# A transformer trunk on one core: V products with the high parts first, one four-bank score tile, a factor from two scalars

## The chip, the core and the metric

The kernel runs on one core of a Trainium2 chip. The metric is the device time of one execution in microseconds (us), taken as the median of several runs. Five engines work side by side, each through its own instructions in order: PE (TensorE, the matrix products), ACT (ScalarE), DVE (VectorE), POOL (GpSimd) and SP (SyncE, which issues the DMAs). They wait for one another by semaphores.

## The reference, cut to what matters

The program is a trunk of two layers over 1024 tokens of width 1024, in fp32. Each layer is a token mixer and a gated feed-forward block (SwiGLU), both behind a modulated RMS norm. The change touches the mixer of the first layer, differential attention, and one helper that both mixers use.

```python
def block(qi):                       # 128 queries, 8 heads, 2 components of width 64
    s = einsum('bqhcd,bkhcd->bhcqk', qi, k)
    p = softmax(s, axis=-1)
    w = p[:, :, 0] - lam * p[:, :, 1]
    return einsum('bhqk,bkhe->bqhe', w, v)
...
o = rmsnorm(o, subln_g) * (1.0 - lam_init)
return o @ w_o
```

The second layer's mixer is grouped-query attention with 8 heads and an ordinary softmax.

## The kernel before

**Products.** An fp32 operand is split into a high and a low part of a shorter type (`split`, L94: ACT casts the high part, another engine subtracts it to get the low one). A product is then three matmuls: high by high, high by low, low by high. That is why a projection tile of 128x512 over 1024 inputs takes 24 matmuls (`mm3`, L105 to L107).

**Units of the first layer's attention.** `layer0_attn` walks 64 units: 8 heads by 8 blocks of 128 queries. A unit has these steps.
- `diff_scores` (L532 on): 12 score matmuls (L548) into two tiles "S" of [128, 1024] fp32, one for each component, two PSUM banks each. Then, for each component, its negated maximum over the keys (L556, DVE), for component 0 a shift by a logarithm (L558, DVE), and the exponential with its row sum (L559, ACT).
- Still in `diff_scores`: the reciprocal of component 1's sum (L563), the factor rho = sum0 * (-lambda) / sum1 (L564), and e0 + rho * e1 in one pass (L565), all on DVE.
- `p_transpose` (L251): two groups of four 128x128 transposes (L256) into a bank "T", and the split of each (ACT cast L95, DVE subtraction L96) into the tiles `pt`.
- `av` (L262), once for two units: 24 matmuls of 256 columns into a half of bank "A" (L268 to L270). For every block k of keys it does V high by P high, V low by P high, V high by P low.
- `subln` (L568), once for four units: A copied to SBUF (L573, ACT), squared (L574), row sums by PE into A (L184), a chain of small operations on four columns (L579 to L589, DVE and one POOL), a broadcast by PE (L190), and the scaled result (L591).

Between these steps the PE computes the next head's Q, K and V projections, 144 matmuls a head into the single bank "M", which ACT evacuates (L470). For Q and K a rotary embedding follows (`rope`: L221 on DVE, L223 to L225 on POOL, then a split). Once a head V is transposed, eight 128x128 blocks (L242). Modulation vectors of the layer come from POOL (L129) and ACT (L130), spread over the units.

**PSUM before.** Eight banks: four in the pool `pss` (two tiles "S"), two "T", one "A", one "M". The two "S" tiles serve one unit; the next unit's scores go into the same two. `issue_after` keeps all other score matmuls of a unit behind its first.

**What sets the order.** The Python code issues the units with a look-ahead of two (`attention`, L272, with the order string "spatpup" for this layer). A scheduler then orders every engine's instructions by priorities (`high_priority` with offsets) and by its own forecast of times, and places the waits by tile: an instruction that reads or writes a tile is ordered against the others that touch that tile. So the order on an engine isn't read from the source, but from the compiled program.

A **turn**, below, is four units, which is half a head: two `av`, one `subln`, 72 projection matmuls. It falls into four stretches, each from the end of one unit's scores to the end of the next unit's. They are called A to D here: in A the second `av` of a group and, once a head, the V transposes; in B the row sums and the first steps of `subln`, then projections; in C the broadcast, projections and the beginning of the next group's first `av`; in D the rest of that `av`, then projections. After the change all 24 products of that `av` stand in C, and D has projections alone beside its transposes.

Of the kernel before, what the change touches and what calls it, by code (L numbers as in the profile page):

```python
# [12 lines left out]
ALU = mybir.AluOpType  # L13
AX = mybir.AxisListType

P = 128
S = 1024
D = 1024
KT = 8
NF = 22  # L20
CH = 512
# [19 lines left out]
PSUM = bass.MemoryType.PSUM  # L41
# [17 lines left out]
class Trunk:  # L59
# [144 lines left out]
    def norm_apply(self, pool, xs, rb, av, bv, hs):  # L204

        nc = self.nc

        def step(d):
            u = self.t(pool, "ft", [P, CH])
            b = bv[:, d:d + 1]  # L210
            nc.vector.scalar_tensor_tensor(out=u, in0=xs[d], scalar=av[:, d:d + 1], in1=rb, op0=ALU.mult, op1=ALU.mult)
            hi, lo = hs[d] = self.hpair()
            nc.scalar.activation(out=hi, in_=u, func=AF.Identity, bias=b, scale=1.0)
            nc.vector.scalar_tensor_tensor(out=lo, in0=u, scalar=b, in1=hi.bitcast(F32), op0=ALU.add, op1=ALU.subtract)  # L214

        return [lambda d=d: step(d) for d in range(KT)]
# [45 lines left out]
    def av(self, v, pt, ps):  # L262
        mm = self.nc.tensor.matmul
        vh, vl = v
        for k in range(KT):
            ks = slice(k * P, (k + 1) * P)
            hi, lo = pt[k // 4][0][:, k % 4, :], pt[k // 4][1][:, k % 4, :]
            mm(ps, lhsT=vh[:, ks], rhs=hi, start=(k == 0), stop=False)  # L268
            mm(ps, lhsT=vl[:, ks], rhs=hi, start=False, stop=False)  # L269
            mm(ps, lhsT=vh[:, ks], rhs=lo, start=False, stop=(k == KT - 1))  # L270

    def attention(self, units, fills, part1, part2, after, order, depth=2):  # L272

# [24 lines left out]
    def run(self):  # L298
        tc, nc, a = self.tc, self.nc, self.a
        with tc.tile_pool(name="cp", bufs=1) as cp, tc.tile_pool(name="sp", bufs=2) as sp, \  # L300
                tc.tile_pool(name="hp", bufs=50) as hp, \
                tc.tile_pool(name="pss", bufs=2, space=PSUM) as pss, \
                tc.tile_pool(name="pst", bufs=2, space=PSUM) as pst, \
                tc.tile_pool(name="psa", bufs=1, space=PSUM) as psa, \
                tc.tile_pool(name="psm", bufs=1, space=PSUM) as psm:
            self.cp, self.sp, self.hp, self.pss = cp, sp, hp, pss
            self.banks = {"T": pst, "A": psa, "M": psm}
            sm = self.sm = cp.tile([P, C_END], F32, name="sm")
            nc.sync.dma_start(out=sm, in_=a["small"])
            self.ident = cp.tile([P, P], F32, name="ident")  # L310
            make_identity(nc, self.ident)
            self.ones = cp.tile([P, 1], F32, name="ones")
            nc.vector.memset(self.ones, 1.0)
            self.nhalf = cp.tile([P, 8], F32, name="nhalf")
            nc.vector.memset(self.nhalf, -0.5)
            self.cond = cp.tile([P, 8], F32, name="cond")
            nc.scalar.activation(out=self.cond, in_=sm[:, C_C:C_C + 8], func=AF.Silu)
            self.mods = [[cp.tile([P, 8], F32, name=f"mod{i}_{j}") for j in range(6)] for i in range(2)]
            self.avec = [[cp.tile([P, 8], F32, name=f"a{i}_{j}") for j in range(2)] for i in range(2)]
            o_dram = [self.dram(f"o{i}") for i in range(2)]  # L320
            x_dram = self.dram("xs")

            with tc.tile_pool(name="wp0", bufs=2) as self.wp, tc.tile_pool(name="cr", bufs=1) as self.cpool:
                hs, proj0 = self.start()
                ow = self.layer0_attn(hs, proj0, o_dram[0])
            hs = self.ffn(0, ow, x_dram)
            with tc.tile_pool(name="wp1", bufs=2, reuse_waits="tile") as self.wp:
                ow = self.layer1_attn(hs, o_dram[1], x_dram)
            self.ffn(1, ow, None)

    def dram(self, name):
        return self.tc.dram_tile([KT, P, S], F32, name=name)

    def start(self):

        nc, a = self.nc, self.a
        m, av = self.mods[0], self.avec[0][0]
        hs = [[None] * KT, [None] * KT]
        S0, S1 = self.t(self.pss, "S"), self.t(self.pss, "S")
        accs = [[S0[:, :CH], S0[:, CH:]], [S1[:, :CH], S1[:, CH:]], [self.bank("T"), self.bank("M")]]  # L340
        with self.tc.tile_pool(name="st", bufs=2) as st, self.tc.tile_pool(name="stx", bufs=8) as stx, \
                self.tc.tile_pool(name="stw", bufs=1) as stw, \
# [189 lines left out]
    def diff_scores(self, q, k, u, ep, s4):  # L532
        nc = self.nc
        es = []
        s1 = self.t(self.sp, "sum", [P, 1])
        sums = [s4[:, u % 4:u % 4 + 1], s1]
        us = slice(u % 4 * P, (u % 4 + 1) * P)
        qh, ql = q[u // 4]
        pss = [self.t(self.pss, "S") for _ in range(2)]
        first = None  # L540

        for n in range(2):
            kh, kl = k[n]
            for i, (x, y) in enumerate(((qh, kh), (qh, kl), (ql, kh))):
                for c in range(2):
                    r = slice(c * 64, c * 64 + 64)
                    with self.tc.issue_after(first.ins) if first else contextlib.nullcontext():
                        ins = nc.tensor.matmul(pss[c][:, n * CH:(n + 1) * CH], lhsT=x[r, us], rhs=y[r, :], start=i == 0, stop=i == 2)  # L548
                    if n == i == 0:
                        first = ins  # L550
        for c in range(2):
            ps = pss[c]
            mx = self.t(self.sp, f"mx{c}", [P, 1])
            e = self.t(ep, "e")
            with self.tc.high_priority(offset=SAHEAD):
                nc.vector.tensor_reduce(out=mx, in_=ps, op=ALU.max, axis=AX.X, negate=True)  # L556
                if c == 0:
                    nc.vector.tensor_scalar(out=mx, in0=mx, scalar1=self.lnbig, scalar2=None, op0=ALU.subtract)  # L558
                nc.scalar.activation(out=e, in_=ps, func=AF.Exp, bias=mx, scale=1.0, accum_out=sums[c])  # L559
            es.append(e)  # L560
        rho = self.t(self.sp, "rho", [P, 1])
        with self.tc.high_priority(offset=SAHEAD):
            nc.vector.reciprocal(out=rho, in_=s1)  # L563
            nc.vector.scalar_tensor_tensor(out=rho, in0=sums[0], scalar=self.neglam, in1=rho, op0=ALU.mult, op1=ALU.mult)  # L564
            nc.vector.scalar_tensor_tensor(out=es[0], in0=es[1], scalar=rho, in1=es[0], op0=ALU.mult, op1=ALU.add)  # L565
        return es[0]

# [181 lines left out]


    def norm_parts(self, ft, bslot, tmp, xs, rb, av, bv, c, h0, ops):

        nc = self.nc
# [449 lines left out]
```

## Time and profile before

| | us |
|---|---|
| median of 3 runs | 2755.31 (2752.56 to 2761.1) |
| the profiled execution, its own time | 2753.28 |
| its span in the trace | 2751.2 |
| PE busy | 2600.1 (95%) |
| DVE busy | 1913.9 (70%) |
| ACT busy | 1193.2 (43%) |
| POOL busy | 988.7 (36%) |

The span is the time between the first and the last instruction in the trace; the execution's own time is 2.1 us longer. The first layer's attention takes about 100 to 745 us of the span, the second layer's about 1560 to 1990 us; the rest is the start and the two feed-forward blocks. Starts in the trace are us from the start of the span. A matmul's duration in the trace overlaps the next one's, so that the pace is read from the starts.

### The profile page before, as it was taken

To read this page: it belongs to the slowest core of one execution; us is meant where nothing else is said; L and a number is where in the kernel's file an instruction comes from. 1 tells how busy PE (TensorE), PEld (TensorE's weight loads), DVE (VectorE), ACT (ScalarE), POOL (GpSimd) and SP (SyncE) were. 2 spreads that over 40 slices of the span, in tenths; PEclk is the share of its full clock that TensorE was granted. 3 is DMA by queue.
4 is the path that set the end of the run, shared out by engine and by line. 5 is a ranking of instruction groups with operands and counts; after the bars stand their busy time and mean duration, and the time that the engine had idled before them with its cause. 6 is when DMAs were issued, how large, how long until landed. Compare 5 with 4: busy or idle time off the path is not lost.

```text
span 2751.2 us, 34376 instructions
## 1 busy us (share of the span) xinstructions
PE 2600.1 (95%) x12888; PEld 2138.1 (78%) x12888; DVE 1913.9 (70%) x2921; ACT 1193.2 (43%) x2049; POOL 988.7 (36%) x664
## 2 busy tenths in 40 slices
PE   6799999999998999999999899999998999999997
PEld 5577777777776888888887788888877888888886
DVE  6777777777667667676666777577567666666666
ACT  5455555555443333333334565555443333332323
POOL 7634444531154223232223456433153222222222
PEclk9899999999998999999999999999999999999998
DMA  6211211112211222221214222213211111111112
GB/s 255 74 44 49 70 50 59 63 42 96 78 49 58 66 65 74 65 69 62 71 64 146 96 73 89 85 59 110 70 35 50 54 50 58 54 50 54 50 58 85
DMA packets 86582, 195.89 MB, mean 71 GB/s; under 512 B 9488, under 2 KB 11792, under 8 KB 86416
## 3 DMA queue, kind: packets, MB, share of 16 engines
q1 hardware_dynamic: 86416, 193.71, 20.7%
q8 instruction: 101, 1.65, 0.3%
q14 instruction: 65, 0.53, 0.1%
HBM read 177.94 MB, written 15.73 MB: 70 GB/s over the span
## 4 chain that ended last, share of the span: by engine, by line
PE 76%; DVE 12%; ACT 3%; POOL 3%; DMA 2%; issue 2%; SPq 0%; DVEq 0%; ACTq 0%; POOLq 0%
PE T L105 7%; PE T L106 7%; PE T L107 7%; PE S L106 6%; PE S L105 6%; PE S L107 6%; PE M L105 6%; PE M L106 5%; PE M L107 5%; PE S L548 3%; PE T L256 3%; PE A L270 2%; PE A L268 2%; PE A L269 2%; DVE mx L556 2%
## 5 line engine op out<-in xcount | busy, mean ns | idle before, releaser
L833 POOL TENSOR_TENSOR raw<-raw,raw 128x512 f32<-128x512 f32 x214 | 299.2, 1399 | 877.5 <-DMA raw<-in_w_in 552.1
L95 ACT CAST whi<-raw 128x512 fp32r<-128x512 f32 x402 | 249.0, 621 | 672.1 <-PE T L106 215.7
L96 DVE TENSOR_TENSOR wlo<-raw,whi 128x512 fp32r<-128x512 f32 x402 | 330.3, 826 | 124.8 <-ACT whi L95 124.4
L105 PE MATMUL M<-h,whi 128*128 128x512 f32 x616 | 252.6, 410 | 8.6 <-ACT tmp L470 4.2
L1036 DVE SCALAR_TENSOR_TENSOR h<-T,mod,h 128x512 f32<-128x512 f32 (+1 forms) x270 | 197.7, 733 | 70.8 <-PE T L107 69.6
L107 PE MATMUL M<-h,wlo 128*128 128x512 f32 x616 | 244.6, 397 | 1.0 <-POOL wlo L96 1.0
L105 PE MATMUL S<-h,whi 128*128 128x512 f32 x572 | 226.7, 397 | 19.5 <-DVE ft L918 19.3
L106 PE MATMUL M<-h,whi 128*128 128x512 f32 x616 | 244.9, 398 | 0.0
L95 ACT CAST pt<-T 128x512 fp32r<-128x512 f32 x256 | 145.3, 588 | 211.5 <-PE T L256 211.0
L106 PE MATMUL S<-h,whi 128*128 128x512 f32 x572 | 227.5, 398 | 5.0 <-DVE h L214 3.1
L96 DVE TENSOR_TENSOR pt<-T,pt 128x512 fp32r<-128x512 f32 x256 | 171.6, 682 | 80.7 <-ACT pt L95 80.4
L107 PE MATMUL S<-h,wlo 128*128 128x512 f32 x572 | 226.2, 396 | 0.0
L105 PE MATMUL T<-g,whi 128*128 128x512 f32 (+1 forms) x540 | 210.7, 390 | 10.2 <-DVE h L1036 8.8
L106 PE MATMUL T<-g,whi 128*128 128x512 f32 (+1 forms) x540 | 208.3, 386 | 1.4 <-DVE g L96 1.4
L107 PE MATMUL T<-g,wlo 128*128 128x512 f32 (+1 forms) x540 | 207.9, 385 | 0.0
L129 POOL TENSOR_TENSOR wraw<-wraw,cond 128x1024 f32<-128x1024 f32 x64 | 155.9, 2437 | 126.9 <-DMA wraw<-in_ada_t 119.6
L556 DVE TENSOR_REDUCE mx<-S 128x1 f32<-128x1024 f32 x128 | 150.2, 1215 | 44.3 <-PE S L548 44.2
L270 PE MATMUL A<-pt,v 128*128 128x256 f32 x512 | 155.6, 304 | 23.2 <-DVE pt L96 23.2
L559 ACT ACTIVATE e<-S,mx 128x1024 f32<-128x1024 f32 x128 | 141.4, 1111 | 71.7 <-DVE mx L558 71.7
L256 PE MATMUL T<-ident,e 128*128 128x128 f32 x1024 | 149.1, 280 | 13.3 <-DVE pt L96 10.1
L268 PE MATMUL A<-pt,v 128*128 128x256 f32 x512 | 156.3, 305 | 4.3 <-ACT pt L95 4.2
L269 PE MATMUL A<-pt,v 128*128 128x256 f32 x512 | 151.4, 296 | 0.0
(290 smaller groups left out, 6445.7 us busy)
## 6 DMA issues: line engine op xcount, KB each, us to landing
raw<-in_w_in SPq DMA_DIRECT2D x200, 256.0 KB, 2.8
wraw<-in_ada_t SPq DMA_DIRECT2D x64, 512.0 KB, 3.2
raw<-in_w_out SPq DMA_DIRECT2D x88, 256.0 KB, 2.6
wraw<-in_wqkvA SPq DMA_DIRECT2D x23, 512.0 KB, 3.2
aq<-in_ada_s SPq DMA_DIRECT2D x16, 512.0 KB, 4.9
raw<-in_ada_w SPq DMA_DIRECT2D x32, 256.0 KB, 2.6
wraw<-in_wqkvB SPq DMA_DIRECT2D x15, 512.0 KB, 3.3
o<-tmp SPq DMA_DIRECT2D x28, 256.0 KB, 2.0
```

The costliest lines, as they stand in the source:

```text
L95: self.nc.scalar.copy(out=hi, in_=src)
L96: (eng or self.nc.vector).tensor_tensor(out=lo, in0=src, in1=hi.bitcast(F32), op=ALU.subtract)
L105: mm(ps, lhsT=whi[:, ws], rhs=xh, start=first and k == 0, stop=False)
L106: mm(ps, lhsT=whi[:, ws], rhs=xl, start=False, stop=False)
L107: mm(ps, lhsT=wlo[:, ws], rhs=xh, start=False, stop=last and k == n - 1)
L256: nc.tensor.transpose(ps[:, i * P:(i + 1) * P], w[:, k * P:(k + 1) * P], self.ident)
L268: mm(ps, lhsT=vh[:, ks], rhs=hi, start=(k == 0), stop=False)
L269: mm(ps, lhsT=vl[:, ks], rhs=hi, start=False, stop=False)
L270: mm(ps, lhsT=vh[:, ks], rhs=lo, start=False, stop=(k == KT - 1))
L556: nc.vector.tensor_reduce(out=mx, in_=ps, op=ALU.max, axis=AX.X, negate=True)
L833: self.nc.gpsimd.tensor_tensor(out=t, in0=x, in1=y, op=op)
L1036: self.nc.vector.scalar_tensor_tensor(out=x, in0=ps, scalar=gate2[:, d:d + 1], in1=x, op0=ALU.mult, op1=ALU.add)
```

## The change

It does three things.

1. `av` issues, for each half of the keys, four products of V high by P high, then four of V low by P high; the eight products with the low part of P come last, after both halves. The number of matmuls stays 24, and the second layer uses the same helper.
2. In the first layer a unit's two score tiles become the two halves of one tile "SS" of [128, 2048] fp32, in a pool `ps0` of one buffer, four banks. The rule that held the score matmuls behind the first (`issue_after`) goes. The pool `pss` with two "S" tiles is opened behind the first layer's attention, for the rest of the program, with its reuse waits by tile. The start of the program takes its accumulators from one "SS".
3. rho is computed by an operation on one tensor with two scalars that are read by pointer (`tensor_scalar`), in place of `scalar_tensor_tensor` with one scalar and two tensors.

```diff
@@ av
+        for half in range(2):
+            for v_ in (vh, vl):
+                for k in range(4 * half, 4 * half + 4):
+                    mm(ps, lhsT=v_[:, k * P:(k + 1) * P], rhs=pt[half][0][:, k % 4, :], start=k == 0 and v_ is vh, stop=False)
         for k in range(KT):
-            ks = slice(k * P, (k + 1) * P)
-            hi, lo = pt[k // 4][0][:, k % 4, :], pt[k // 4][1][:, k % 4, :]
-            mm(ps, lhsT=vh[:, ks], rhs=hi, start=(k == 0), stop=False)
-            mm(ps, lhsT=vl[:, ks], rhs=hi, start=False, stop=False)
-            mm(ps, lhsT=vh[:, ks], rhs=lo, start=False, stop=(k == KT - 1))
+            mm(ps, lhsT=vh[:, k * P:(k + 1) * P], rhs=pt[k // 4][1][:, k % 4, :], start=False, stop=k == KT - 1)
@@ run
-                tc.tile_pool(name="pss", bufs=2, space=PSUM) as pss, \
...
+            with tc.tile_pool(name="ps0", bufs=1, space=PSUM) as self.ps0, tc.tile_pool(name="wp0", bufs=2) as self.wp, \
+                    tc.tile_pool(name="cr", bufs=1) as self.cpool:
                 hs, proj0 = self.start()
                 ow = self.layer0_attn(hs, proj0, o_dram[0])
...
+            with tc.tile_pool(name="pss", bufs=2, space=PSUM, reuse_waits="tile") as self.pss:
...
+    def scores2(self):
+
+        t = self.t(self.ps0, "SS", [P, 2 * S])
+        return t[:, :S], t[:, S:]
@@ diff_scores
-        pss = [self.t(self.pss, "S") for _ in range(2)]
-        first = None
+        pss = self.scores2()
...
-                    with self.tc.issue_after(first.ins) if first else contextlib.nullcontext():
-                        ins = nc.tensor.matmul(pss[c][:, n * CH:(n + 1) * CH], lhsT=x[r, us], rhs=y[r, :], start=i == 0, stop=i == 2)
-                    if n == i == 0:
-                        first = ins
+                    nc.tensor.matmul(pss[c][:, n * CH:(n + 1) * CH], lhsT=x[r, us], rhs=y[r, :], start=i == 0, stop=i == 2)
...
-            nc.vector.scalar_tensor_tensor(out=rho, in0=sums[0], scalar=self.neglam, in1=rho, op0=ALU.mult, op1=ALU.mult)
+            nc.vector.tensor_scalar(out=rho, in0=rho, scalar1=sums[0], scalar2=self.neglam, op0=ALU.mult, op1=ALU.mult)
```

In the new source the lines of the softmax are two further down: the maximum is L558, the shift L560, the exponential L561, rho L566, the score matmul L552, the copy of A L575, the evacuation of M L476.

The compiled order shows what moves. First DVE, in a stretch A of the first layer; `mx` is a component's maximum, `S` or `SS` the score tile, `pt` the low part of P. Before:

```order
L556 TENSOR_REDUCE mx_599_2868<-S_2854 128x1 [waits PE_49]
L556 TENSOR_REDUCE mx_601_2873<-S_2855 128x1 [waits PE_49]
L558 TENSOR_SCALAR mx_599_2868<-mx_599_2868,lam 128x1 [waits DVE_49]
L96 TENSOR_TENSOR pt_2913<-T_2979,pt_2912 128x4x128 [waits Activation_49]
L96 TENSOR_TENSOR pt_2915<-T_2992,pt_2914 128x4x128 [waits Activation_49]
L563 RECIPROCAL rho_2877<-sum_2853 128x1 [waits Activation_49]
```

After:

```order
L558 TENSOR_REDUCE mx_573_2842<-SS_2829 128x1 [waits PE_49]
L96 TENSOR_TENSOR pt_2887<-T_2952,pt_2886 128x4x128 [waits Activation_49]
L560 TENSOR_SCALAR mx_573_2842<-mx_573_2842,lam 128x1 [waits DVE_49]
L96 TENSOR_TENSOR pt_2889<-T_2965,pt_2888 128x4x128 [waits Activation_49]
L558 TENSOR_REDUCE mx_575_2847<-SS_2829 128x1 [waits Activation_49]
```

The second maximum waited for PE and stood right behind the first; now it waits for ACT, and the instruction it waits for is component 0's exponential on the same tile.

ACT in a stretch A without V, after the change (`e` is an exponential, `A_3231` the result of `av`):

```order
L95 CAST pt_3256<-T_3337 128x4x128 [waits PE_49]
L95 CAST pt_3258<-T_3350 128x4x128 [waits PE_49]
L561 ACTIVATE e_3213,s_639_3197<-SS_3199,mx_642_3212 128x1024 [waits DVE_49]
L575 COPY tmp_3436<-A_3231 128x512 [waits PE_49]
L561 ACTIVATE e_3218,sum_3198<-SS_3199,mx_644_3217 128x1024 [waits DVE_49]
```

The copy of A, which stood behind both exponentials, stands between them.

PE in a stretch A with the V transposes (L242), before:

```order
L270 MATMUL A_2887<-pt_2915,v_2347 128x256
L548 MATMUL S_2946<-h_2644,h_2434 128x512 [waits Activation_49]
L268 MATMUL A_2887<-pt_2914,v_2347 128x256
L269 MATMUL A_2887<-pt_2914,v_2348 128x256
L270 MATMUL A_2887<-pt_2915,v_2347 128x256
L242 MATMUL T_3106<-ident,vz_2929 128x128 [waits PE_49]
...
L548 MATMUL S_2947<-h_2644,h_2434 128x512 [waits Activation_49]
L548 MATMUL S_2946<-h_2645,h_2434 128x512
```

PE in a stretch A after the change:

```order
L268 MATMUL A_3231<-pt_3258,v_3076 128x256 x3
L268 MATMUL A_3231<-pt_3258,v_3077 128x256 x4
L270 MATMUL A_3231<-pt_3257,v_3076 128x256 [waits DVE_49]
L270 MATMUL A_3231<-pt_3257,v_3076 128x256 x3
L270 MATMUL A_3231<-pt_3259,v_3076 128x256 [waits DVE_49]
L270 MATMUL A_3231<-pt_3259,v_3076 128x256 x3
L552 MATMUL SS_3305<-h_2621,h_2531 128x512 [waits PE_49,Activation_49]
L552 MATMUL SS_3305<-h_2621,h_2531 128x512
L552 MATMUL SS_3305<-h_2622,h_2531 128x512 x2
```

One score matmul stood among the V products, ahead of the other eleven (31 times in the program); now all twelve stand together, behind the second exponential of the unit before. The products with P low (L270) are the last eight.

PE in a stretch D after the change, at the edge of two projection tiles in the bank M:

```order
L105 MATMUL M_3297<-h_610,whi_3293 128x512
L106 MATMUL M_3297<-h_611,whi_3293 128x512
L107 MATMUL M_3297<-h_610,wlo_3294 128x512
L105 MATMUL M_3405<-h_352,whi_3293 128x512 [waits Activation_49]
L106 MATMUL M_3405<-h_353,whi_3293 128x512
```

The last three matmuls of one tile and the first of the next, which waits for ACT's evacuation of the single bank M (L476), follow directly; before, a unit's transposes or scores stood between two tiles here.

## Rows read from the trace of the kernel before

**Rows 1.** The page: busy us (share of the span) and instructions of each engine.
```profile
PE 2600.1 (95%) x12888; PEld 2138.1 (78%) x12888; DVE 1913.9 (70%) x2921; ACT 1193.2 (43%) x2049; POOL 988.7 (36%) x664
```

**Rows 2.** PE's waits in 130:790; line waited for: us in total, times, longest.
```profile
PE A L270 <- DVE pt L96: 17.0, 13, 1.4
PE S L548 <- ACT e L559: 9.1, 8, 2.6
...
PE T L256 <- DVE e L565: 2.3, 4, 0.8
```

**Rows 3.** PE timeline, scores ten turns apart: start, us, engine, line, operation, tiles, count.
```profile
214.16 0.50 PE L548 MATMUL S<-h,h 64*128 64x512 f32 x2
...
611.79 0.50 PE L548 MATMUL S<-h,h 64*128 64x512 f32 x2
```

**Rows 4.** PE timeline, the beginning of a stretch A; in brackets idle time and releaser.
```profile
411.98 1.66 PE L548 MATMUL S<-h,h 64*128 64x512 f32 x12
413.57 1.09 PE L256 MATMUL T<-ident,e 128*128 128x128 f32 x8
...
416.80 0.39 PE L270 MATMUL A<-pt,v 128*128 128x256 f32 x1 [1.40 <-DVE pt L96]
```

**Rows 5.** PE timeline, a score matmul alone among V products.
```profile
441.00 0.28 PE L269 MATMUL A<-pt,v 128*128 128x256 f32 x1
441.12 0.28 PE L270 MATMUL A<-pt,v 128*128 128x256 f32 x1
441.33 0.49 PE L548 MATMUL S<-h,h 64*128 64x512 f32 x1
441.75 0.39 PE L268 MATMUL A<-pt,v 128*128 128x256 f32 x1
441.97 0.28 PE L269 MATMUL A<-pt,v 128*128 128x256 f32 x1
```

**Rows 6.** 23 projection matmuls, three stretches A: us, busy by engine, granted clock, DMA.
```profile
435.29:440.53 5.24, 5.24 (x25) 4.32 (x23) 5.24 (x9) 1.71 (x5) 4.00 (x4) 1.00 0.37 129
...
413.57:424.25 10.68, 9.04 (x54) 7.50 (x53) 6.48 (x10) 6.46 (x13) 2.35 (x1) 0.84 0.15 52
453.78:463.49 9.71, 8.08 (x47) 6.30 (x45) 7.61 (x9) 5.52 (x10) 4.34 (x3) 0.82 0.18 57
613.38:621.63 8.25, 6.61 (x46) 5.12 (x45) 5.34 (x8) 4.82 (x9) 0.00 (x0) 1.00 0.01 3
```

**Rows 7.** DVE timeline: a softmax in A, and one step of `subln` in B.
```profile
413.67 2.35 DVE L556 TENSOR_REDUCE mx<-S 128x1 f32<-128x1024 f32 x2 [1.52 <-PE S L548]
415.95 0.20 DVE L558 TENSOR_SCALAR mx<-mx,lam 128x1 f32<-128x1 f32 x1
416.07 1.28 DVE L96 TENSOR_TENSOR pt<-T,pt 128x512 fp32r<-128x512 f32 x2
...
469.71 1.22 DVE L586 TENSOR_SCALAR sv<-sv 128x4 f32<-128x4 f32 x1
```

**Rows 8.** ACT timeline in the same stretch A.
```profile
418.75 1.10 ACT L559 ACTIVATE e<-S,mx 128x1024 f32<-128x1024 f32 x1
...
422.69 0.59 ACT L573 COPY tmp<-A 128x512 f32<-128x512 f32 x1
...
424.17 0.61 ACT L470 ACTIVATE tmp<-M 128x512 f32<-128x512 f32 x1
```

**Rows 9.** Lines L558 and L564: duration in ns, least/median/most; first and last start.
```profile
L558 DVE TENSOR_SCALAR mx<-mx,lam x64: 193/204/218, 100.7 to 719.6; 128x1 f32<-128x1 f32 x64
...
L564 DVE SCALAR_TENSOR_TENSOR rho<-s,lam,rho x64: 207/219/2373, 104.8 to 722.5; 128x1 f32<-128x1 f32 x64
```

**Rows 10.** PE's waits in 0:135, for the evacuation of M.
```profile
PE M L105 <- ACT tmp L470: 4.2, 2, 2.6
```

**Rows 11.** PE's waits in 1560:2035, the second layer's attention.
```profile
PE T L256 <- DVE pt L96: 5.2, 6, 2.9
PE A L270 <- DVE pt L96: 4.8, 7, 1.5
```

More of the change, by code (lines that the diff above doesn't have):

```diff
@@ L305, in run @@
                 tc.tile_pool(name="psm", bufs=1, space=PSUM) as psm:
-            self.cp, self.sp, self.hp, self.pss = cp, sp, hp, pss
+            self.cp, self.sp, self.hp = cp, sp, hp
             self.banks = {"T": pst, "A": psa, "M": psm}
@@ L321, in run @@
             x_dram = self.dram("xs")
-            with tc.tile_pool(name="wp0", bufs=2) as self.wp, tc.tile_pool(name="cr", bufs=1) as self.cpool:
+            with tc.tile_pool(name="ps0", bufs=1, space=PSUM) as self.ps0, tc.tile_pool(name="wp0", bufs=2) as self.wp, \
+                    tc.tile_pool(name="cr", bufs=1) as self.cpool:
                 hs, proj0 = self.start()
                 ow = self.layer0_attn(hs, proj0, o_dram[0])
[L326 to L329, printed above, removed]
+            with tc.tile_pool(name="pss", bufs=2, space=PSUM, reuse_waits="tile") as self.pss:
+                hs = self.ffn(0, ow, x_dram)
+                with tc.tile_pool(name="wp1", bufs=2, reuse_waits="tile") as self.wp:
+                    ow = self.layer1_attn(hs, o_dram[1], x_dram)
+                self.ffn(1, ow, None)
     def dram(self, name):
         return self.tc.dram_tile([KT, P, S], F32, name=name)
+    def scores2(self):
+        t = self.t(self.ps0, "SS", [P, 2 * S])
+        return t[:, :S], t[:, S:]
     def start(self):
@@ L338, in start @@
         hs = [[None] * KT, [None] * KT]
-        S0, S1 = self.t(self.pss, "S"), self.t(self.pss, "S")
+        S0, S1 = self.scores2()
         accs = [[S0[:, :CH], S0[:, CH:]], [S1[:, :CH], S1[:, CH:]], [self.bank("T"), self.bank("M")]]
```

## Prediction

> **What bounds the kernel now.** The page's first row [rows 1] is read first: PE is busy for 2600.1 of 2751.2 us, so in most of the program the end is set by PE's work, and the change removes no matmul. It can only win or lose what PE idles, what PE loses at changes between kinds of matmul, and what it loses to a lower clock. So the next view is PE's waits in the first layer's attention [rows 2]. The largest is the wait of the V products for P's low part: 17.0 us in 13 waits, 1.3 each. Next are the scores' waits for the exponentials that still read their banks, 9.1 us in 8. Both are waits that the change touches. The unit of account is a turn of four units: from 214.16 to 611.79 are ten of them [rows 3], (611.79 - 214.16) / 10 = 39.76 us each. About 13 of the 16 turns run in this steady pattern; the first and the last ones I hold at before's value.
>
> The third loss is the clock. Three stretches A of one turn each [rows 6] show it: 8.25 us at a granted clock of 1.00, but 9.71 at 0.82 and 10.68 (with V's eight transposes) at 0.84. The dips come after the wait of 1.40 us for P low [rows 4], during which PE does nothing: then part of the stretch runs at the lower level, 1.2 in place of 2.4 GHz. Like against like, a dip costs 9.71 - 8.25 = 1.46 us. Going through the eleven turns by the same view I count seven with a dip, 7 / 11 x 1.46 = 0.93 us a turn.
>
> **What the change removes, in a turn of 39.76 us.**
> - V products: with the low parts last, P low is subtracted while sixteen products with the high parts run, at 0.12 us each [rows 5], 1.9 us. The two subtractions take 1.28 us [rows 7] and end before. The 17.0 us go: 17.0 / 13 = 1.31 a turn.
> - Lone score matmuls. From 441.12 to 441.97 [rows 5] is 0.85 us for two V products and one score matmul. Two steps of 0.12 and a twelfth of the 1.59 from the scores' start to the next kind [rows 4], 0.13, make 0.37; the rest, 0.48, is paid for changing the kind twice. Two in a turn, all gone: 0.96.
> - The scores' waits of before belong to the old chain and are replaced: 9.1 / 13 = 0.70.
> - The dips, taken out for now: 0.93.
>
> That leaves 39.76 - 1.31 - 0.96 - 0.70 - 0.93 = 35.86 us.
>
> **What it adds.** The compiled order shows what the diff doesn't: the waits go by tile, and with both components in one tile the maximum of component 1 waits for the exponential of component 0, and its own exponential for that maximum. Before, the chain from the scores' end to free banks was two maxima (2.35), the shift (0.20) and two exponentials (1.10 each) [rows 7, 8]: with hand-overs of about 0.1 to 0.2, 5.1 us. Now it is maximum 1.18, shift 0.20, exponential 1.10, maximum 1.18, exponential 1.10, with five hand-overs of 0.1 to 0.2: 5.5. And other work has slipped into it. The next unit's twelve score matmuls wait for all of it; before, the matmuls of component 0 needed the first half only. Where PE has other work for so long, nothing is lost; so stretch by stretch:
> - A: ahead of the next scores PE has only eight transposes (0.9 us), 24 V products (24 x 0.12 = 2.9, and 0.1 at each change) and once a head V's eight transposes (0.9): 4.1, or 5.0 us. The chain: first maximum over at 1.3, a subtraction of P low (0.64) ahead of the shift, shift over at 2.1, first exponential over at 3.3, second maximum at 4.5. Meanwhile ACT has taken up the copy of A (0.59 [rows 8]), which waits for the V products' end at about 4.1 to 4.4 and delays the second exponential to about 4.95; it ends at 6.2, and the scores start at 6.35. PE idles 6.35 - 4.1 = 2.2 us; with V the new casts on ACT push the chain about as far as V's own work, 2.1 to 2.6. I take 2.2.
> - B: the old e-combination, a shuffle and six small `subln` operations stand on DVE between the shift and the second maximum. One of these has taken 1.22 us on four columns [rows 7], where an operation as small takes 0.20. With the e-combination and the shuffle (some 2 us) and one or two such steps the chain of 5.5 becomes 7.4 to 8.1 us. PE's work there is 19 to 24 projection matmuls at 5.24 / 23 = 0.23 us [rows 6], the transposes and the small products: 6 to 7. That is 1 to 2.2 idle; I take 1.5.
> - C: some 26 projection matmuls (5.9 us) and an `av` (3.0) cover the chain; nothing is added there.
> - D: the 24 projection matmuls cover the chain too. But the next tile in M follows the last directly, and PE waits for ACT's evacuation: not less than its 0.61 [rows 8], not more than 2.6, the longest such wait at the start [rows 10]. ACT is free when it comes, so I take the lower end and two hand-overs: 1.0.
>
> Sum: 35.86 + 2.2 + 1.5 + 1.0 = 40.56 us, without any dip. The dips come back: they followed an idle time of 1.40 us, and A has a longer one in every turn now, and B one as long. At before's rate, 0.93, a turn takes 41.5, which is 1.73 more than 39.76; 13 turns: +22.5 us.
>
> **The rest.** rho: the new form is like the shift, an operation with pointer scalars on one column, 193 to 218 ns in all 64 cases, where the old one took 207 to 2373 [rows 9]. DVE gains some 17 us, but PE waited for the e-combination behind it for 2.3 us in all [rows 2]; I count nothing, at most -2. The bound on the other side is that the new form is held up as the old one was: then nothing changes. Second layer: the V products wait there for P low for 4.8 us in 7 waits, and the transposes 5.2 us for the subtraction that frees their bank [rows 11]. The first go; the second stay or grow, as the subtractions aren't earlier. With the dips that followed some of them I take -5 (-10 to +3). The start and the feed-forward blocks keep their order: 0. The sum is +22.5 - 5 = +17.5 us on the profiled execution's 2753.3; the median of before lies 2.0 us above that execution, so the forecast of the median is 2755.3 + 17.5 = 2773, and I give 2772.
>
> **A rule weighed.** The rows show dips of the clock behind single waits of 1.40 us [rows 4, 6]. The Trainium skill, "TensorE: Matmul & The Clock Gate", section "A second HAM failure mode: psum-queue depth-cycling", says that a kernel which cycles through its PSUM banks, so that PE idles for short moments between groups of matmuls, can see the clock go up and down all the time. The trace agrees with it in that short waits sufficed in seven of eleven turns. It speaks against this change, which puts such a moment behind nearly every unit; the last rival is that case. The skill's "PSUM — Partial Sum Buffer", section "PSUM bank collisions raise a hardware error", speaks the other way: two engines may read different banks at once, so nothing in the chip asks for the second maximum to wait for the first exponential. The compiled order has the wait all the same; no run here shows the chip without it.
>
> **The rivals.**
> - *Even.* The idle times are as summed, but the dips vanish, because the waits lie elsewhere: 40.56 a turn, +0.8 x 13 - 5 = +5, 2760. For it: B's and D's waits are split from A's by long work at full rate. Against it: A's idle time is longer than the one that did it before.
> - *Faster.* DVE and ACT keep the chain under PE's work in B, and M's evacuation is done in time. Then a turn takes 35.86 + 2.2 = 38.1 and with some dips (0.5) 38.6: -1.2 x 13 = -15; with 0.3 a turn from the transitions and the e-combination, and -8 in the second layer, -27: 2728. If A were covered too, the whole of the four terms removed would be gained, 3.9 x 13 + 8 = 59, 2697; the chain of 5.5 against 4.1 us of work speaks against it. For the rival: the sizes in B are the least certain of the sum, and POOL isn't always busy there.
> - *Slower by more.* Every idle time in A and B ends in a dip: two a turn, 2.92 in place of 0.93: +3.7 x 13 - 5 = +43, 2798. It decides as soon as the waits in B do what A's did. Against it: work that then has slack hides part of the lower pace.
> - *The change doesn't do what it says*: the low parts' subtractions come so late on DVE, behind the serial chain, that the V products wait as before. In A they stand ahead of the second maximum, so this is not seen in the order; it would add 1.3 x 13 = 17 us to the forecast and lies within the last rival.
>
> **How the numbers follow.** A measurement of this kernel tells about 0.3% from no change, 8.3 us: faster is under 2747, slower over 2763.6. Chances: the forecast 0.46, 2772 with its own range of 2764 to 2784; even 0.22; faster 0.20; slower by more 0.12. Faster 0.20, same 0.24, slower 0.56. The range takes the forecast, the even case, nearly all of the slower one and the upper edge of the faster one: 2738 to 2798.
>
> **What would show it.** PE's waits in the first layer's attention should have no line for P low worth a microsecond, and a new largest one, scores waiting for ACT's exponential, of some 45 us in 25 waits or more; M waiting for its evacuation, some 13 us. The DVE timeline should show the two maxima of a unit apart, with an idle time that ends on the exponential. Turns should be 41 to 42 us, and stretches A near 8 us at full clock, B near 9.5 to 10, scores included. A page with PE's clock at 0.98 or more in 300:700 would make the even case right; a turn under 39.3 would make the forecast wrong, and B's chain would be the step at fault.

## The result and the profile after

The changed kernel takes 2795.43 us (median of 4 runs, 2793.26 to 2799.04) beside 2753.93 us of the kernel before: a ratio of 1.0149, with a 95% interval of 1.0135 to 1.0163, or about 41 us more. The forecast had the sign and less than half of the size (+17).

The page of the changed kernel, beside [rows 1]:

```profile
PE 2583.5 (92%) x12888; PEld 2129.3 (76%) x12888; DVE 1924.7 (69%) x2921; ACT 1198.4 (43%) x2049; POOL 994.0 (36%) x664
```

PE has the same 12888 matmuls and is even busy for 17 us less, but the span has grown from 2751.2 to 2794.5 us. So the loss is time in which PE stands still. From the start to the first score matmul it is 4.2 us longer (96.37 against 92.17), and from there to the last one of the first layer 45.6 (671.18 against 625.56). But the two kernels don't do the same work in that time: the changed one has 48 matmuls more there, which before stood behind the attention. So the loss is read at equal work. PE has the same 4201 matmuls behind it, inside the first feed-forward block, at 863.61 us before (first row) and at 909.80 after (second row):

```profile
0.00:863.61 863.61, 780.39 (x4201) 621.76 (x4202) 636.97 (x1041) 447.35 (x776) 379.20 (x244) 0.94 0.22 76
```

```profile
0.00:909.80 909.80, 766.25 (x4201) 614.43 (x4202) 649.54 (x1041) 450.04 (x776) 383.19 (x244) 0.94 0.21 72
```

That is 46.2 us for the start and the attention. What follows is 2.9 us shorter, which makes the 43.3 us between the spans.

Next, ten turns of the changed kernel, from the score matmul at 224.94 to that at 652.39 (start, us, operation, tiles, count):

```profile
224.94 0.50 PE L552 MATMUL SS<-h,h 64*128 64x512 f32 x2
...
652.39 0.50 PE L552 MATMUL SS<-h,h 64*128 64x512 f32 x2
```

(652.39 - 224.94) / 10 = 42.75 us a turn, against 39.76 [rows 3], with the same number of matmuls in both. PE's waits in these ten turns (line waited for: us in total, times, longest):

```profile
PE SS L552 <- ACT e L561: 23.1, 12, 4.0
PE M L105 <- ACT vz L476: 8.1, 5, 2.3
PE M L105 <- ACT tmp L476: 7.9, 4, 2.8
PE A L190 <- DVE sr L591: 5.5, 6, 1.7
```

And in the ten turns of the kernel before:

```profile
PE A L270 <- DVE pt L96: 14.0, 10, 1.4
PE A L268 <- ACT pt L95: 2.4, 10, 0.2
PE T L256 <- DVE e L565: 2.3, 4, 0.8
PE S L548 <- ACT e L559: 0.7, 2, 0.4
```

The 14.0 us for P low are gone, as forecast. In their place stand 23.1 us for the exponentials, 16.0 for the evacuation of the single bank M, 5.5 for `subln`, and 7.9 in smaller waits (4.7 before).

A stretch A without V, in DVE's timeline of the changed kernel, shows the serial softmax (in brackets idle time and releaser):

```profile
397.38 1.22 DVE L558 TENSOR_REDUCE mx<-SS 128x1 f32<-128x1024 f32 x1 [0.67 <-PE SS L552]
...
399.18 0.20 DVE L560 TENSOR_SCALAR mx<-mx,lam 128x1 f32<-128x1 f32 x1
...
400.66 1.23 DVE L558 TENSOR_REDUCE mx<-SS 128x1 f32<-128x1024 f32 x1 [0.68 <-ACT e L561]
```

The two maxima, 2.35 us in one piece in [rows 7], stand apart, and the second waits for ACT. ACT then copies A and comes to the second exponential, and the next scores begin at 403.51, 6.25 us after the last ones ended at 397.26:

```profile
401.76 0.59 ACT L575 COPY tmp<-A 128x512 f32<-128x512 f32 x1 [1.14 <-PE A L270]
402.25 1.12 ACT L561 ACTIVATE e<-SS,mx 128x1024 f32<-128x1024 f32 x1
```

```profile
403.51 0.73 PE L552 MATMUL SS<-h,h 64*128 64x512 f32 x4 [1.78 <-ACT e L561]
```

That is the stretch as forecast (6.35 us). What was not forecast is a stretch A with V. PE first, then ACT, DVE and POOL, 435.67 to 449:

```profile
435.67 1.66 PE L552 MATMUL SS<-h,h 64*128 64x512 f32 x12
...
442.73 0.60 PE L242 MATMUL T<-ident,vz 128*128 128x128 f32 x4
447.30 2.31 PE L552 MATMUL SS<-h,h 64*128 64x512 f32 x10 [3.96 <-ACT e L561]
```

```profile
437.66 1.06 ACT L130 ACTIVATE wraw<-wraw 128x1024 f32<-128x1024 f32 x1 [4.11 <-POOL wraw L129]
...
440.16 1.11 ACT L561 ACTIVATE e<-SS,mx 128x1024 f32<-128x1024 f32 x1 [0.39 <-DVE mx L560]
...
444.52 1.06 ACT L130 ACTIVATE wraw<-wraw 128x1024 f32<-128x1024 f32 x1 [1.47 <-POOL wraw L129]
...
445.57 0.57 ACT L575 COPY tmp<-A 128x512 f32<-128x512 f32 x1
446.04 1.12 ACT L561 ACTIVATE e<-SS,mx 128x1024 f32<-128x1024 f32 x1
```

```profile
441.40 1.22 DVE L558 TENSOR_REDUCE mx<-SS 128x1 f32<-128x1024 f32 x1 [0.67 <-ACT e L561]
```

```profile
442.12 2.37 POOL L129 TENSOR_TENSOR wraw<-wraw,cond 128x1024 f32<-128x1024 f32 x1 [4.49 <-DMA wraw<-in_ada_t]
```

The second maximum was over at 442.6 (it began at 441.40 and took 1.22), and ACT had ended a cast of V at 443.05. It could have gone on with the copy of A and the second exponential then. But its queue is in order, and a modulation sum (L130) stands ahead: it waits 1.47 us for POOL's product, and that for a DMA. The second exponential starts at 446.04, and PE idles for 3.96 us.

Not every stretch with V is like this. Of the five in the ten turns, two have a sum in this place and idle for 3.96 and 3.98 us. The other three have none there and idle for 1.35 or 1.36, as here:

```profile
536.54 1.66 PE L552 MATMUL SS<-h,h 64*128 64x512 f32 x12 [1.35 <-ACT e L561]
```

Such a sum stands also ahead of M's evacuation in a stretch D, here PE and ACT:

```profile
477.96 0.54 PE L105 MATMUL M<-h,whi 128*128 128x512 f32 x1 [2.23 <-ACT tmp L476]
```

```profile
475.78 1.06 ACT L130 ACTIVATE wraw<-wraw 128x1024 f32<-128x1024 f32 x1 [1.72 <-POOL wraw L129]
...
477.31 0.60 ACT L476 ACTIVATE tmp<-M 128x512 f32<-128x512 f32 x1
```

The third thing is the clock. The stretch with V, 435.67 to 447.30, and the one behind it (us, busy by engine, granted clock, DMA share, GB/s):

```profile
435.67:447.30 11.63, 6.69 (x54) 5.67 (x54) 4.57 (x7) 6.69 (x13) 4.32 (x2) 1.00 0.20 62
447.30:460.00 12.70, 12.70 (x50) 10.16 (x50) 11.34 (x22) 5.53 (x10) 4.80 (x4) 0.60 0.07 29
```

Behind the wait of 3.96 us most of a whole stretch runs at the lower level, 1.2 GHz.

### The profile page after: what moved, and what is told of

It is laid out like the page before. It is cut to its first block, busy times and chain, and to the rows that moved or that the text cites. A ratio compares the mean times of both kernels' runs of the same rounds, so it can differ in the third digit from the quotient of the medians.

```text
span 2794.5 us, 34324 instructions
## 1 busy us (share of the span) xinstructions
PE 2583.5 (92%) x12888; PEld 2129.3 (76%) x12888; DVE 1924.7 (69%) x2921; ACT 1198.4 (43%) x2049; POOL 994.0 (36%) x664
## 5 line engine op out<-in xcount | busy, mean ns | idle before, releaser
L95 ACT CAST whi<-raw 128x512 fp32r<-128x512 f32 x402 | 249.6, 622 | 669.9 <-PE T L106 215.6
L96 DVE TENSOR_TENSOR wlo<-raw,whi 128x512 fp32r<-128x512 f32 x402 | 336.2, 841 | 126.2 <-ACT whi L95 125.6
L105 PE MATMUL M<-h,whi 128*128 128x512 f32 x616 | 257.9, 419 | 43.5 <-ACT tmp L476 19.0
L106 PE MATMUL M<-h,whi 128*128 128x512 f32 x616 | 249.6, 405 | 0.0
L105 PE MATMUL S<-h,whi 128*128 128x512 f32 x556 | 220.3, 397 | 22.4 <-DVE ft L920 22.1
L106 PE MATMUL S<-h,whi 128*128 128x512 f32 x556 | 220.8, 397 | 5.3 <-DVE h L214 3.4
L107 PE MATMUL S<-h,wlo 128*128 128x512 f32 x556 | 219.6, 395 | 0.0
L95 ACT CAST pt<-T 128x512 fp32r<-128x512 f32 x256 | 144.3, 587 | 153.4 <-PE T L256 152.7
L558 DVE TENSOR_REDUCE mx<-SS 128x1 f32<-128x1024 f32 x128 | 156.1, 1220 | 78.1 <-PE SS L552 52.0
L561 ACT ACTIVATE e<-SS,mx 128x1024 f32<-128x1024 f32 x128 | 143.2, 1119 | 93.6 <-DVE mx L558 38.9
L105 PEld LDWEIGHTS M<-h,whi 128*128 128x128 f32 x616 | 120.9, 196 | 76.5 <-ACT tmp L476 22.1
L96 POOL TENSOR_TENSOR wlo<-wraw,whi 128x1024 fp32r<-128x1024 f32 (+1 forms) x31 | 68.1, 2199 | 250.7 <-ACT whi L95 216.5
L268 PE MATMUL A<-pt,v 128*128 128x256 f32 x1024 | 142.3, 287 | 9.6 <-ACT pt L95 7.6
```

The source lines that it names most:

```text
L95: self.nc.scalar.copy(out=hi, in_=src)
L96: (eng or self.nc.vector).tensor_tensor(out=lo, in0=src, in1=hi.bitcast(F32), op=ALU.subtract)
L105: mm(ps, lhsT=whi[:, ws], rhs=xh, start=first and k == 0, stop=False)
L106: mm(ps, lhsT=whi[:, ws], rhs=xl, start=False, stop=False)
L107: mm(ps, lhsT=wlo[:, ws], rhs=xh, start=False, stop=last and k == n - 1)
L268: mm(ps, lhsT=v_[:, k * P:(k + 1) * P], rhs=pt[half][0][:, k % 4, :], start=k == 0 and v_ is vh, stop=False)
```

## Experiments

All ratios are to the kernel before, run on the same chip in the same session, with 95% intervals; 1% is 27.5 us. The expectations in us were made beside 2754 for the kernel before. It took 2756 to 2760 in these sessions, so a ratio is compared with them as that share of 2754. Each edit also changes the compiled order beyond what it is meant to change.

### The parts alone

The three edits apart, and the first and third together:

```diff
 av_only         V products in the new order (as in the change)
 tile_only       one "SS" tile, no issue_after, pss behind the first layer (as in the change)
 rho_only        rho by two scalars (as in the change)
 av_rho          the change with two "S" tiles and issue_after
```

> The kernel before with only the V products in the new order; two score tiles and the old rho stay. Theory (the four-bank tile costs, through its serial softmax): the waits for P low go, 1.3 us a turn, and with them most of the clock's dips that followed them (0.9 a turn), some 2 to 5 us in the second layer: 2725 to 2738 us. Rival (the new order of the V products costs, because it moves an av into another stretch and leaves the scores nothing to hide behind): 2765 us or more, nearly all of the change's +41.

> The kernel before with only the four-bank score tile; old order of the V products and old rho. Theory: the loss of the change and what the V products gave are both seen, so 2795 plus 10 to 25: 2805 to 2820 us. Rival (the V products cost): within 10 us of before, 2745 to 2765.

> The kernel before with only rho by two scalars. Theory: off the path, -2 to 0 us, 2752 to 2754 of 2754. Rival (shorter DVE work moves the order elsewhere): more than 6 us either way.

> The changed kernel with two score tiles again (V products in the new order and rho by scalars stay). Theory: as the V products alone, 2723 to 2738 us, faster than both kernels. Rival (V products cost): 2765 or more.

| kernel | ratio | about, us |
|---|---|---|
| rho_only | 0.9999 (0.9987 to 1.0011) | 0 |
| av_only | 0.9963 (0.9948 to 0.9979) | -10 |
| av_rho | 0.9923 (0.9905 to 0.9942) | -21 |
| tile_only | 1.0072 (1.0046 to 1.0098) | +20 |
| the change | 1.0149 (1.0135 to 1.0163) | +41 |

rho_only and av_rho came out as expected. av_only gained less than expected, and tile_only lost less: about 2774 us in place of 2805 to 2820. The V order gains, the tile loses. With the V order alone the waits for P low go, and others take their place, so that its ten steady turns take 39.80 us each (from the scores at 211.02 to those at 609.02), no less than before. PE's waits in av_only from 130 to 770 show the new ones:

```profile
PE S L548 <- ACT e L559: 11.8, 14, 2.6
PE M L105 <- ACT vz L470: 4.3, 2, 2.2
PE M L105 <- ACT tmp L470: 4.1, 6, 0.7
```

And the parts don't add up. Tile and V order with rho would make about 0; together they make +41. In the presence of the new V order the tile costs 1.0149 - 0.9923, some 62 us, three times what it costs alone. So most of the loss comes of the two together.

av_rho is faster than both kernels. rho by itself gave nothing; beside the new V order it seems to give another 0.4%, with intervals that almost touch. The compiled order differs there too (34 lone score matmuls in place of 39), so it was not the operation's own time that was shown to matter.

### The serial softmax

max_first keeps the one tile and takes the serial order away, by issuing both maxima ahead of both exponentials. two_serial keeps two tiles and makes the softmax serial, through one small tile that both maxima use:

```diff
 max_first (against the change)
+        for c in range(2): reduce(mxs[c], pss[c])
+        shift(mxs[0])
+        for c in range(2): exp(es[c], pss[c], mxs[c])
 two_serial (against av_rho)
+        mx = self.t(self.sp, "mx0", [P, 1])
         for c in range(2):
             ps = pss[c]
-            mx = self.t(self.sp, f"mx{c}", [P, 1])
```

> The changed kernel with both maxima (and the shift) issued ahead of both exponentials, so that the second maximum no longer waits for the first exponential; the tile stays one of four banks. Theory (the serial softmax is most of what the tile costs): 2750 to 2768 us, 25 to 45 under the changed kernel's 2795. Rival (the twelve scores behind the whole unit's release are the cost): the tile is still released in one piece, so 2780 us or more.

> Two score tiles, new V order and new rho, but both components' maxima go into one small tile, so that the second maximum waits for the first exponential, as in the changed kernel. Theory (serial softmax): 2765 to 2785 us, against 2739 without this wait. Rival (release in one piece): 2738 to 2750.

max_first: 1.0042 (1.0027 to 1.0057); one more execution of the same kernel, under the label max_lag, took 2766.18 us.

> One more look at the changed kernel with both maxima ahead of both exponentials: 2766 to 2775 us if the earlier figure stands.

two_serial: 1.0120 (1.0104 to 1.0135). So to take the serial wait out of the changed kernel gives back 1.07%, 29 us of its 41; and to put it into two tiles costs 1.97%, 54 us, and makes a kernel about as slow as the changed one, without any four-bank tile. The serial softmax is shown to be a cause in both directions. Both runs came out as the theory had it and not as the rival, two_serial a little above the range. What the tile costs beyond it is max_first against av_rho, 1.2%.

### The modulation sums in ACT's queue

```diff
 after_nosum, before_nosum (the change, the kernel before), layer 0 alone
-                nc.scalar.activation(out=w, in_=w, func=AF.Copy, accum_out=dst[:, d:d + 1])
+                nc.gpsimd.memset(dst[:, d:d + 1], 1.0)
 after_nodma (the change), layer 0 alone
-            nc.sync.dma_start(out=w, in_=self.a["ada_t"][layer, j - 2, d])
-                nc.gpsimd.tensor_tensor(out=w, in0=w, in1=cond, op=ALU.mult)
+                nc.gpsimd.tensor_tensor(out=w, in0=cond, in1=cond, op=ALU.mult)
 after_lag, av_rho_lag (the change, av_rho): the sum of step d - 1 issued ahead of step d's DMA
```

> The changed kernel without the first layer's modulation sums on ACT (left out: the 32 accumulating passes; their results are set to one, so the output isn't the reference's). POOL's products and the DMAs stay. Theory (these sums stand in ACT's queue ahead of the second exponential and of the evacuation of M, and wait there for POOL and a DMA): the 4.1 us ahead of the scores in turns with V fall to 1.4 to 1.9, the 2.4 us ahead of M to 1.25, and some dips go: 2768 to 2782 us. Rival (these waits have another cause): 2788 or more.

> The same left out of the kernel before, as the control. Theory: the sums are covered there, 2746 to 2756 us beside 2754. Rival (the sums cost in both alike): as much gained as in the changed kernel, 2740 or less.

> The changed kernel, with the first layer's modulation sums issued one step later: a sum comes ahead of the next step's DMA, so that POOL's product is long done when ACT reaches it. All work stays. Theory (the sums cost because ACT waits in them for POOL and a DMA, in order, ahead of the second exponential and of M's evacuation): most of the gain without the sums, 2768 to 2782 us. Rival (it was the sums' own 1.06 us on ACT, or the order that went with them): 2788 or more.

> Two score tiles, new V order, new rho, and the late sums. Theory (with two tiles the chain is covered and the sums are as well): within 6 us of 2739. Rival (the sums are a cost of their own): 2730 or less.

> The changed kernel with the first layer's modulation weights not loaded (left out: the 32 DMAs; POOL multiplies a resident row by itself, so the output isn't the reference's). POOL's products and ACT's sums stay, 1.06 us each. Theory (ACT waits in the sums for POOL, which waits for a DMA that waits for the buffer of an earlier sum): ratio to before 1.002 to 1.008, most of the gain that leaving out the sums gave (1.0032 against 1.0149). Rival (the sums' own time and place in ACT's queue): 1.012 or more.

after_nosum: 1.0032 (1.0020 to 1.0045). before_nosum: 1.0001 (0.9988 to 1.0014). The same sums, 32 passes of 1.06 us, cost nothing in the kernel before and 1.17%, 32 us, in the changed one. The gain is larger than expected. All six stretches with V from 130 to 700 now idle for 1.35 us or less, where three of six had 3.96 to 4.26. But that is the smaller part. The same ten turns, from 218.08 to 628.65, take 41.06 us each, where they took 42.75. PE's waits in them:

```profile
PE SS L555 <- ACT e L564: 24.6, 18, 2.7
PE M L105 <- ACT vz L479: 8.5, 5, 2.3
...
PE A L271 <- ACT pt L95: 1.7, 7, 0.2
PE A L193 <- DVE sr L594: 1.5, 2, 0.9
PE M L105 <- ACT tmp L479: 1.4, 2, 0.7
```

The scores wait as long in all as with the sums (24.6 against 23.1), in more and shorter waits. What falls is M's wait for the evacuation of Q and K (`tmp`), from 7.9 to 1.4, the one for `subln`, from 5.5 to 1.5, and the one of the V products for the casts of P (`pt`), from 5.1 to 1.7. M's waits for the evacuation of V (`vz`) stay, up to 2.3 us each: there no sum stands ahead on ACT, but a cast of a weight's high part (L95, 1.06 us). Of the 1.69 us a turn, 1.06 are PE's idle time. Another 0.34 at most is the clock: 23.9 us at the lower level in these turns against 30.7, and half of the difference is the most that it can cost.

after_lag: 1.0119 (1.0091 to 1.0148), which tells nothing. The scheduler put the late sums next to POOL's products again, and ACT's waits show the same idle time ahead of them, here in the changed kernel and in after_lag, 130 to 770:

```profile
ACT wraw L130 <- POOL wraw L129: 56.8, 22, 6.7
```

```profile
ACT wraw L129 <- POOL wraw L137: 57.4, 22, 6.8
```

The expectation for after_lag was missed without being tested: the edit didn't bring the order that it was made for. av_rho_lag, 0.9921 (0.9901 to 0.9941), is the same as av_rho; ACT waits there for POOL as in av_rho, so it tells no more.

after_nodma: 1.0057 (1.0040 to 1.0074), as the theory had it. With the DMAs gone and every product and sum still there, 0.92% of the 1.17% come back. So most of what the sums cost goes with the DMAs. That it is the wait and not the place is not shown by this run, because the sums have moved on ACT: none stands ahead of the second exponential in a stretch with V any more, and five stand there in stretches without V. These five give a price for a sum that hardly waits. The sum at 223.74 waits for nothing, and the scores behind it idle for 2.52 us, where a stretch without V in the changed kernel has 1.78:

```profile
226.51 0.73 PE L553 MATMUL SS<-h,h 64*128 64x512 f32 x4 [2.52 <-ACT e L562]
```

That is 0.74 us for a sum without a wait, and 3.96 - 1.35 = 2.61 for the one at 444.52, which waits 1.47 and takes 1.06. Why the DMA comes late there is read from the trace only: the buffers of the weights are two, the sum at 437.66 frees one at 438.8, the load takes 3.2 us by the page, and POOL starts at 442.12.

### The same queue with the other softmaxes

The sums left out of max_first and of two_serial, with the edit of after_nosum:

> The changed kernel with both maxima ahead of both exponentials, and without the first layer's modulation sums (left out, their results set to one, so the output isn't the reference's). Theory (what the four-bank tile still costs there, 1.0042 against 0.9923, is the same queue: sums ahead of both exponentials): 0.992 to 0.997. Rival (it is the release of all four banks in one piece): 1.001 or more.

> Two score tiles with the serial softmax, without the first layer's modulation sums (left out as before). Theory (a serial softmax lays the path on ACT's queue, whatever the tiles): 0.997 to 1.005 against 1.012 with the sums. Rival (on two tiles the serial softmax costs by itself): 1.009 or more.

max_nosum: 0.9947 (0.9932 to 0.9962), as the theory had it and 0.95% less than max_first. So without the sums the four-bank tile is within 0.24% of av_rho, with intervals that overlap. Most of what the tile still cost there needs this queue, and the release of four banks in one piece can't be the whole of it. What av_rho would gain without its sums was not run; two kernels with two tiles gained nothing (before_nosum) or next to nothing (two_serial_nosum, below). The rows of max_first agree: both exponentials stand behind a sum.

```profile
508.53 1.06 ACT L130 ACTIVATE wraw<-wraw 128x1024 f32<-128x1024 f32 x1 [4.89 <-POOL wraw L129]
...
509.59 1.09 ACT L561 ACTIVATE e<-SS,mx 128x1024 f32<-128x1024 f32 x1
```

In av_rho the sum stands at the same place, ahead of both exponentials, but its product is ready sooner (ACT waits in these sums for 25.8 us in all, 56.1 in max_first):

```profile
489.59 1.06 ACT L130 ACTIVATE wraw<-wraw 128x1024 f32<-128x1024 f32 x1 [1.14 <-POOL wraw L129]
```

two_serial_nosum: 1.0115 (1.0098 to 1.0132), by the ratio the same as with the sums. Here the theory fell: on two tiles the serial softmax costs nearly all of its 54 us without this queue. The traces show a part that the ratio hides: the ten steady turns fall from 44.05 to 42.20 us each, but only some 9 us of that are left at the end of the profiled executions. In two_serial the first of a unit's score matmuls is let in after the first exponential, and the other eleven wait for the second. 58 units have such a lone score matmul (59 without the sums), where av_rho has 34, and PE runs at a mean clock of 0.95 from 130 to 700 us in two_serial (first row), against 0.98 in av_rho (second):

```profile
130.00:700.00 570.00, 523.55 (x2876) 409.63 (x2876) 413.69 (x667) 284.80 (x500) 223.30 (x138) 0.95 0.17 55
```

```profile
130.00:700.00 570.00, 546.97 (x3179) 432.89 (x3180) 447.29 (x739) 308.73 (x548) 228.93 (x142) 0.98 0.18 58
```

How the 54 us divide between these lone matmuls, the waits and the clock was not measured apart.

### The rule that holds the scores together

```diff
 av_rho_nohold (against av_rho)
-                    with self.tc.issue_after(first.ins) if first else contextlib.nullcontext():
-                        ins = nc.tensor.matmul(pss[c][:, n * CH:(n + 1) * CH], ...)
+                    nc.tensor.matmul(pss[c][:, n * CH:(n + 1) * CH], ...)
```

> Two score tiles, new V order, new rho, but without the rule that holds a unit's score matmuls behind its first. Theory (that rule is not what the tile's cost comes from): 2730 to 2750. Rival (the rule's removal is part of the change's loss): 2755 or more.

0.9990 (0.9978 to 1.0002): without the rule the gain of av_rho is lost. PE hardly waits, and it is slower all the same. Its row for 130 to 700:

```profile
130.00:700.00 570.00, 567.03 (x3065) 446.15 (x3066) 426.59 (x722) 301.91 (x535) 232.40 (x140) 0.99 0.17 57
```

PE is busy for 567.03 of 570 us at a clock of 0.99, and gets 3065 matmuls done where av_rho gets 3179. The result lies between the theory and the rival. In its order the scores stand in smaller groups, 61 of them of six, as many as one component has. A group of six takes 312.95 - 311.36 = 1.59 us:

```profile
311.36 1.66 PE L547 MATMUL S<-h,h 64*128 64x512 f32 x6
312.95 0.50 PE L106 MATMUL M<-h,whi 128*128 128x512 f32 x1
```

Twelve in a row, which alternate between the components, take just as long: 413.57 - 411.98 in [rows 4]. So a score matmul costs double in such a group. An estimate from these rows is 61 x 1.59 / 2 = 48 us more for the scores, against some 20 us less idle time (PE's waits from 130 to 700 come to 4.2 us, in av_rho to 24.7). That leaves some 28 us, more than the 18 between the two kernels, so the groups are cause enough. That it is the pairing of the components was read from the order and the times, and not tested by itself. It is no part of the change's loss: with the one tile the twelve stand together in all 64 units.

## Why the prediction was right or wrong, point by point

- **The mechanism was right in kind.** The waits for P low are gone, the maxima wait for the exponentials, the scores wait for ACT, M's edge waits for its evacuation. The scores wait in fewer and longer waits than I gave: 36.0 us in 15 from 130 to 790, against some 45 in 25. Stretch A without V came out at 6.25 us to the next scores (6.35 forecast), and the ten stretches A of the steady turns idle for 2.1 us in the mean (2.2 forecast). rho came out at nothing.
- **The step that failed is the one that has ACT free.** For M's edge I wrote that ACT is free when it comes, and took 1.0 us a turn; 1.6 were measured. Nowhere does the sum have a term for the modulation sums in ACT's queue, which wait for POOL and a DMA. The waits were in view in the trace of before, in places where they cost nothing, and I did not price them where the change puts them. after_nosum shows that 32 of the 41 us need these sums, while before_nosum shows that they cost nothing before. With the sums they are spread over M's wait for `tmp`, `subln`, the casts of P, three of the six stretches with V, and the clock. Without them the steady turn is 41.06 us.
- **The turn was mis-sized: 42.75 us measured, 41.5 forecast.** Half of that is one term. I took 0.70 us a turn off for the scores' waits of before, 9.1 us in 8 waits [rows 2] divided by 13 turns. But in the ten steady turns these waits come to 0.7 us, 0.07 a turn; the rest lay at the start and the end of the attention. That is 0.63 us a turn that was never there to be removed. P low was 1.40 in place of 1.31, which gives 0.09 back. Some 0.3 a turn more is not placed.
- **The sum of the added idle time was right by luck.** Forecast were 2.2 + 1.5 + 1.0 = 4.7 us a turn. Measured are 2.3 for the scores, 1.6 for M, 0.55 for `subln` and 0.8 for smaller waits. That is 5.25, or 4.8 without the 0.47 that were there before. M's part is too small in the forecast and stretch B's too large: of its 1.5 there are 0.2 for the scores and 0.55 as a wait of the broadcast for `subln` (5.5 us in 6 waits). Stretch A with V is 2.4 in the mean (2.1 to 2.6 forecast), but as a mixture of 1.35 and 3.97 that was not foreseen.
- **The dips.** I took them at before's rate. The time at the lower level is 23.9 us in the ten turns of before and 30.7 in those of the changed kernel. Half of the difference, 0.34 us a turn, is the most that this can cost.
- **The turns that I held at before's value** at the start and the end of the attention, and the start of the program, were longer too. At equal work the loss up to the end of the attention is 46.2 us: 29.9 in the ten turns, 4.2 at the start, 12.1 in the other turns.
- **The rest**, -5 forecast, was -2.9: P low's waits in the second layer fell from 4.8 [rows 11] to 2.4, the transposes' from 5.2 to 4.4.

So of the 25.8 us that the forecast of +17.5 missed in the profiled execution (43.3), 16.4 lie in the size of the 13 turns, 4.2 in the start, 3.1 in the turns held and 2.1 in the rest. The rival "slower by more" named nearly the right time, 2798, by another mechanism: two dips in each turn. They did not come; in the ten turns the clock's share is about a tenth of what was lost.

## What to carry to other kernels

One tile is one object to a scheduler that places waits by tile: two readers of different halves, on different engines, become a chain, and the compiled order shows it before any run. A longer chain through an in-order engine costs more than its own operations, because every instruction that stands in that queue and waits for something slow can now lie on the path; price those at their wait as well as their duration. And a wait that is to be removed is counted in the turns to which the sum is applied, not in a wider window and divided.

## What the runs showed of the hardware

- A dip of the clock does not follow every wait of PE. The stretch that begins at 395.67 in the changed kernel has a wait of 1.78 us, and 395.67 to 435.67 runs at a granted clock of 1.00 throughout:

```profile
395.67:435.67 40.00, 35.99 (x217) 28.44 (x216) 28.30 (x48) 20.07 (x35) 12.74 (x8) 1.00 0.13 46
```

  Behind a wait of 2.80 us at 564.94 the clock stays at 1.00 as well, for the next 25 us. Waits of 1.40 us were followed by dips in seven of eleven turns before ([rows 4] has one of the waits, [rows 6] three of the stretches), and one of 3.96 us by a stretch at a mean of 0.60. The Trainium skill, "TensorE: Matmul & The Clock Gate", section "A second HAM failure mode: psum-queue depth-cycling", holds short idle moments between groups of matmuls responsible for a clock that goes up and down. The runs agree only in part: tile_only waits for its banks in nearly every turn, and its mean clock from 130 to 700 us is 0.98, above the 0.96 of the kernel before and the 0.95 of the change, in this order:

```profile
130.00:700.00 570.00, 509.56 (x3068) 411.39 (x3068) 420.02 (x709) 300.54 (x527) 223.60 (x141) 0.98 0.18 58
```

```profile
130.00:700.00 570.00, 540.70 (x3123) 432.62 (x3122) 431.62 (x731) 306.26 (x541) 223.72 (x142) 0.96 0.17 58
```

```profile
130.00:700.00 570.00, 492.87 (x2872) 395.50 (x2873) 407.86 (x668) 286.93 (x503) 223.75 (x138) 0.95 0.16 56
```

- A PE that never waits can be the slower one. Six score matmuls of 64 rows in a row took 1.59 us in av_rho_nohold, as long as twelve of two components in turn [rows 4], and a kernel at 99% busy lost a gain of 0.7%. A lone one among products of 128 rows costs 0.48 us beyond its own share in [rows 5].
